# Moving the gates' exponentials between the recurrence's exponentials and its roots, and the input norm's sums and scale to fixed chunks

## The chip, the cores and the metric

One core of one Trainium2 chip runs the whole kernel in one launch. The metric is device time in microseconds (us) of one execution; the time of a kernel is the median of its runs. The engines have short names below: PE is TensorE's matmul, PEld its weight load, DVE VectorE, ACT ScalarE, POOL GpSimd and SP SyncE. Each engine works through its own instructions in the order that was fixed when the program was built; an instruction that waits holds everything behind it on that engine.

## The reference

One inference step of a one-layer hybrid decoder, for a prompt of 256 tokens and 8 sample tokens (264 columns together, model width 2048):

```python
x = x + W_out[ RGLRU-group(xn) || mLSTM-group(xn) ],  xn = RMSNorm(x)   # ONE projection xn @ w_in
x = x + CrossAttn(RMSNorm(x), memory K/V)     # 4 heads, 256 memory tokens
x = x + SwiGLU(RMSNorm(x))
y = RMSNorm_final(x)
```

The two groups matter here. The recurrence (RG-LRU) takes 1024 channels through a causal convolution of width 4, two block-diagonal projections with sigmoids (r and i), and then

```python
log_a = -RG_C * r * softplus(-lam);  a = exp(log_a)
mult = sqrt(max(1 - exp(2 * log_a), 0))
h[t] = a[t] * h[t-1] + mult[t] * (i[t] * xr[t])          # a scan over the tokens
```

The mLSTM group has 4 heads. Its input and forget gates (logi, logf = log_sigmoid) become a running sum and a running maximum over the tokens; the stabilised weights exp(...) are applied to q, k and v. For the 8 sample tokens each head reads a stored matrix memory C (128 x 256), decays it, adds a rank-one update and multiplies it with q; the new C is an output. The head outputs are normalised by a denominator and a per-head RMSNorm.

## The kernel before

**Tiling.** Activations lie transposed: channels on the 128 partitions, the 264 tokens on the free axis, so that a tile of 128 channels is 128 x 264. Weights stream from memory as blocks of 128 output channels: one *step* of the main loop (the list `steps`) is one block of 2048 weights per partition in two halves of 1024. All products of the trunk keep nearly full fp32 accuracy: a weight half (tile `raw`) is copied by ACT to a rounded high part and DVE subtracts to get the remainder (both in tile `W`, four buffers, so two steps), and each chunk of 128 input channels takes three matmuls (`mm3`: high x high, high x low, low x high). A step has 16 chunks, 48 matmuls of 264 columns.

**Steps.** Steps 0 to 3 are the first four output blocks of the recurrence's input, arranged by quarters of the input channels so that PE can begin before all of x is there; they accumulate in four PSUM banks held from the start, two with the tag `ax` (`first[0]`, `first[1]`) and two with the tag `mm` (`first[2]`, `first[3]`). There are four banks of each tag; the steps take theirs from `mm`, side work from `ax`. Steps 4 to 7 are the other four blocks of the recurrence's input, step 8 the gates (a narrow block, 32 matmuls), steps 9 to 16 q and k, 17 to 24 v, 25 to 32 the recurrence's output gate (gelu), 33 to 40 the mLSTM's output gate (sigmoid), then the output projection, the cross-attention and the feed-forward part, which the change doesn't touch.

**Input norm.** The norm's factor per token (`rstd`) is applied when a step's bank is emptied, so PE may run ahead of it, as far as banks go. `square` (line 1317) makes the squares of x on ACT in four quarters and adds them on DVE to `acc_x`. `first_norm` then lets PE sum over the partitions (`token_sums`, six small matmuls), DVE compute the inverse root (`rsqrt`, twelve small dependent instructions), PE spread the result over the partitions (`spread`, six small matmuls) and ACT copy it to `rstd`. After that `evac_first` empties the first four banks.

**Who sets the order.** A step's own code is written out in turn: the weight halves of the next step at high priority, the matmuls, then the evacuation of the step before at raised priority. Side work is written as Python generators (`rg_gen` the recurrence, `ml_gates`, `ml_prompt`, `ml_values`, `ml_heads`, `ml_sample`, `ml_norm`), each with a priority number; `pump` lets them go on after each step, lowest number first, as long as the planner's running prices of DVE and ACT (`price_dve`, `price_act`) stay under PE's price plus `SLACK`. `yield STEP` gives up until the next step. A negative priority runs regardless. A list scheduler then places the instructions of each engine from this text, by priority and its own idea of when each is ready; `tc.issue_after(ins)` forces what it encloses behind `ins` in the order of `ins`'s engine, without a wait for its end.

**Drips.** `later(f, after=n)` hands over small PE work: `drip` is called after every chunk of a projection and issues one waiting function once n chunks have gone by; the next chunk is put behind it with `issue_after`. A function's own countdown begins only when it is at the head of the list.

**The chain of the side work.** `rg_gen` takes one channel block per step: convolution, then in the next step the two projections and sigmoids; then sixteen exponentials (two per block), the products, two square roots over four blocks each, eight scans, and the output DMAs on POOL. `ml_gates` starts when step 8 is emptied: one exponential, a logarithm as a series of some fourteen DVE instructions (`log1p`), two scans, a 4 x 16 exponential (`x16`), a few small PE transposes and products, and the exponential `emc`. In the kernel before, its first exponential stands behind the recurrence's last sigmoid (`rg["last"]`) and `x16` behind the recurrence's second root (`rg["root"]`). `ml_sample` begins when the gates are done: it writes its rows to memory and reads them back spread over the partitions, and then works through 32 units (4 heads x 8 samples), each two ACT products, one DVE update of C and two DVE dot products. `ml_norm` follows when heads and samples are done; its sums (24 small matmuls) are drips too.

ACT keeps one set of function tables at a time; sigmoid, exponential, square root and gelu each bring an `ACT_TABLE_LOAD` in this kernel when the one before was of another set.

Of the kernel before, what the change touches and what calls it, by code (L numbers as in the profile page):

```python
# [17 lines left out]
P = 128  # L18
# [4 lines left out]
N = T + NS  # L23
# [60 lines left out]
def layer_kernel(ctx: ExitStack, tc, xT, memT, vec, wrg, w_in, w_out, w_q, w_k, w_v, w_o,  # L84
# [138 lines left out]
    st = {}  # L223
# [51 lines left out]
    def drip(all=False):  # L275
        while drips and (all or drips[0][0] <= 0):
            k = drips[0]
            with tc.high_priority():
                st["drip"] = k[1].pop(0)()
            if not k[1]:  # L280
                drips.pop(0)
            if not all:
                return
        if drips:
            drips[0][0] -= 1
# [61 lines left out]
    def spread(ps, c, n=N):  # L347

        for j in range(2 if n == T else 3):
            lo, hi = (j * P, j * P + P) if j < 2 else (T, N)  # L350
            pe.matmul(ps[:, lo:hi], c[j].to_broadcast([P, P]), ident[:, P - (hi - lo):], start=True, stop=True)

    def rstd_from(acc, y, n, keep=None):

# [100 lines left out]

    def evac_rgx(n):
        def f(ps):
            if n == 0:
                rg["xr"] = Arr(RGB)
            z = B([P, 2, 292])  # L460
            zi = z[:, 0, :]
            dve.memset(zi[:, 0:3], 0.0)
            smp = zi[:, 259:291].rearrange("p (b j) -> p b j", j=4)
            hist = V("cst", n * 24, 24).rearrange("p (b j) -> p b j", j=3)
            act.activation(smp[:, :, 0:3], hist, AF.Copy)
            dve.tensor_mul(zi[:, 3:259], ps[:, :T], rstd[:, :T])
            dve.tensor_mul(smp[:, :, 3:4], ps[:, T:N].rearrange("p (b j) -> p b j", j=1),
                           rstd[:, T:N].rearrange("p (b j) -> p b j", j=1))
            rg["z", n] = z
            rg["zn"] = n + 1  # L470
        return f

    def rg_conv(n):
# [15 lines left out]
    def rg_gen():  # L489
        wr = [B([P, 8, P]), B([P, 8, P])]  # L490
        for j in range(2):
            sp.dma_start(wr[j], wrg[:, j * 8: j * 8 + 8, :])
        r, ig = Arr(RGB), Arr(RGB)
        for n in range(RGB):
            while rg["zn"] <= n:
                yield STEP
            rg_conv(n)
            yield STEP
            for t, j, b in ((r, 0, "ba"), (ig, 1, "bx")):
                ps = bank("ax")  # L500
                pe.matmul(ps[:, :N], wr[j][:, n, :], rg["xr"](n), start=True, stop=True)
                last = act.activation(t(n), ps[:, :N], AF.Sigmoid, bias=V(b, n))
            yield 0.1
        yield STEP
        xr, c = rg["xr"], rg["c"]
        e2 = Arr(RGB)

        rg["last"] = last
        for q in range(2):
            for n in range(4 * q, 4 * q + 4):  # L510
                with tc.issue_after(last.ins):
                    act.activation(e2(n), r(n), AF.Exp, scale=c[:, 8 + n: 9 + n])
                    le = act.activation(r(n), r(n), AF.Exp, scale=c[:, n: n + 1])
            dve.tensor_scalar(e2.tile(q), e2.tile(q), 1.0, -1.0, op0=OP.min, op1=OP.add)
            dve.tensor_mul(ig.tile(q), ig.tile(q), xr.tile(q))
            yield 2.0
        for q in range(2):
            with tc.issue_after(le.ins):
                rg["root"] = act.activation(e2.tile(q), e2.tile(q), AF.Sqrt, scale=-1.0)
            dve.tensor_mul(ig.tile(q), ig.tile(q), e2.tile(q))  # L520
            yield 1.2
        h = Arr(RGB)
        rg["h"] = h
        for n in range(RGB):
            dve.tensor_tensor_scan(h(n)[:, :T], r(n)[:, :T], ig(n)[:, :T], 0.0, op0=OP.mult, op1=OP.add)
            yield 0.6
        h0 = V("h0", 0, 64).rearrange("p (n b) -> p n b", b=NS)
        for q in range(2):
            hq, rq_, iq = (t.tile(q)[:, :, T:N] for t in (h, r, ig))
            dve.tensor_mul(hq, rq_, h0[:, 4 * q: 4 * q + 4, :])  # L530
            dve.tensor_add(hq, hq, iq)
            act.activation(hlast[:, 4 * q: 4 * q + 4, :], h.tile(q)[:, :, T - 1: N], AF.Copy)
        pool_e.dma_start(o_h, hlast)
        pool_e.dma_start(o_cp, cpo)
        pool_e.dma_start(o_cs, cso)
        yield 0.3
# [49 lines left out]
    def ml_gates():  # L586
        R = ml["R"]
        li, u, e, lf, b, g, M = (R(j)[0:4] for j in range(7))
        yield STEP
        dve.scalar_tensor_tensor(e, u, -1.0, u, op0=OP.mult, op1=OP.min)  # L590
        while "last" not in rg:
            yield STEP
        with tc.issue_after(rg["last"].ins):
            act.activation(e, e, AF.Exp)
        yield 0.4
        log1p(lf, e)
        yield 6.0
        dve.tensor_scalar(u, u, 0.0, None, op0=OP.min)
        dve.tensor_sub(lf, u, lf)

        one = ones[0:4, 0:1].to_broadcast([4, T])
        dve.tensor_tensor_scan(b[:, :T], one, lf[:, :T], 0.0, op0=OP.mult, op1=OP.add)
        dve.tensor_sub(g[:, :T], li[:, :T], b[:, :T])
        dve.tensor_tensor_scan(M[:, :T], g[:, :T], g[:, :T], 0.0, op0=OP.max, op1=OP.max)
        dve.tensor_add(b[:, :T], b[:, :T], M[:, :T])
        dve.tensor_scalar(M[:, :T], M[:, :T], -1.0, None, op0=OP.mult)
        dve.tensor_copy(mrow[:, 0:1], b[:, T - 1: T])

        s = slice(T, N)
        dve.tensor_add(lf[:, s], lf[:, s], V("m0", 0, 8)[0:4])  # L610
        dve.tensor_max(b[:, s], lf[:, s], li[:, s])
        dve.tensor_copy(mrow[:, 1:], b[:, s])
        x16 = e[:, 0:16]
        dve.tensor_sub(x16[:, 0:8], lf[:, s], b[:, s])
        dve.tensor_sub(x16[:, 8:16], li[:, s], b[:, s])
        pool_e.dma_start(o_m, mrow)
        yield 3.0
        while "root" not in rg:
            yield STEP
        with tc.issue_after(rg["root"].ins):  # L620
            act.activation(x16, x16, AF.Exp)
        yield STEP
        ps = bank("ax")
        i4 = ident[0:4, 0:4]
        for j in range(2):
            pe.transpose(ps[:, 64 + 4 * j: 68 + 4 * j], g[:, j * P: j * P + P], i4)
        for j, w0 in enumerate(WIN):
            pe.transpose(ps[:, 72 + 4 * j: 76 + 4 * j], b[:, w0: w0 + P], i4)
        for h in range(H):
            pe.matmul(ps[:, h * 16: h * 16 + 16], ident[0:4, h: h + 1].to_broadcast([4, P]), x16,  # L630
                      start=True, stop=True)
        act.activation(bcs, ps[:, 0:64].rearrange("p (h j) -> p h j", j=16), AF.Copy)
        act.activation(gcol, ps[:, 64:72].rearrange("p (j h) -> p j h", h=H), AF.Copy)
        act.activation(emc, ps[:, 72:84], AF.Exp, scale=-1.0)
        yield 0.1

    def evac_qk(j):
# [232 lines left out]
    def proj(src, rhs, evac, cols=2048, n=N, need=()):  # L870

        def f(i):
            ps = bank()
            w = W(i)
            nch = cols // P
            for c in range(nch):
                d = st.pop("drip", None)
                if d is None:
                    mm3(ps[:, :n], w(c), rhs(c), c == 0, c == nch - 1)
                else:  # L880
                    with tc.issue_after(d.ins):
                        mm3(ps[:, :n], w(c), rhs(c), c == 0, c == nch - 1)
                drip()
            return ps
        steps.append((src, cols, f, evac, need))
# [11 lines left out]
        return f  # L897

    def evac_first(_):
        for n in range(4):  # L900
            evac_rgx(n)(first[n])

    for q in range(4):
        steps.append((w_in[q], 2048, pe_first(q), evac_first if q == 3 else None, ()))
# [409 lines left out]
    def square(q):  # L1314
        s = B([P, 4, N])
        act.activation(s, xres[:, 4 * q: 4 * q + 4, :], AF.Square)
        if q == 0:
            sq["t"] = s
            return
        dve.tensor_add(sq["t"], sq["t"], s)  # L1320
        if q == 3:
            t = sq["t"]
            dve.tensor_add(t[:, 0:2, :], t[:, 0:2, :], t[:, 2:4, :])
            dve.tensor_add(acc_x, t[:, 0, :], t[:, 1, :])

    def first_norm():
        ps = bank("ax")
# [5 lines left out]
            rsqrt(v, r)  # L1333
            return i

        k = later(sums, after=8)
        while k[1]:
            yield STEP
        spread(ps, [r[:, j: j + 1] for j in range(3)])
        act.activation(rstd, ps[:, :N], AF.Copy)  # L1340
        yield 0.1

    pend = []
    for i, (src, cols, pef, evf, need) in enumerate(steps):
# [21 lines left out]
                    square(q)  # L1366
        if i == 3:
            fn = side(first_norm(), -1)
        if i == 4:
            with tc.issue_after(st["split"].ins), tc.issue_after(st["low"].ins):  # L1370
                rg_coef()
        if evf is not None:
# [120 lines left out]
```

## Time and profile before

| | before |
|---|---|
| median of 3 runs (lowest, highest) | 1569.76 us (1567.02, 1570.49) |
| the profiled execution: time, span | 1570.7 us, 1568.9 us |
| granted TensorE clock, mean over the span | 0.991 |
| PE busy, share of the span | 1541.4 us, 98% |
| DVE busy, ACT busy | 1057.5 us, 780.7 us |
| ACT_TABLE_LOAD | 10, 1283 ns each |

How to read the rows: a row of a timeline has the start in us from the span's beginning, the duration, the engine, the line, the operation, out<-in by the program's tile names, the shape and a count; in square brackets stands the idle time before it and the engine whose work ended that idle time. Nearly all rows have line L63, since the engines are wrapped in a helper that records every operation there; tiles tell them apart: `W` and `raw` are weights, `mm` and `ax` the PSUM banks, `t` and `B` working buffers, `c` small columns, `rgc` the recurrence's coefficients, `bcs` the samples' decay factors. A row of the windows view gives, for a stretch of time, its length and the busy time (and instructions) of PE, PEld, DVE, ACT and POOL, then the granted TensorE clock, the DMA engines' busy share and GB/s.

### The profile page before, as it was taken

The numbers are of one execution on the slowest core, as the hardware profiler recorded it, in microseconds if no ns is written. First come the engines' busy times: TensorE is split into PE (matmuls) and PEld (weight loads), VectorE is DVE, ScalarE is ACT, GpSimd is POOL, SyncE is SP. The second block draws the span as 40 slices with busy tenths as digits, with TensorE's granted clock in tenths as the row PEclk, the third lists the DMA queues.
The fourth block names the chain that finished last, engine by engine and source line by source line (L and its number), as shares of the span: only waits on it lengthen the run. The fifth ranks groups of instructions, "written<-read, shape, count | busy, mean of one in ns | idle before, by whom it ended". The sixth has DMA issues, their size and how long they took to land.

```text
span 1568.9 us, 30102 instructions
## 1 busy us (share of the span) xinstructions
PE 1541.4 (98%) x12094; PEld 1506.0 (96%) x12094; DVE 1057.5 (67%) x1996; ACT 780.7 (50%) x1227; POOL 123.1 (8%) x190
## 2 busy tenths in 40 slices
PE   9999997999999999999999999999999999999997
PEld 9999997999999888889999999999999999999997
DVE  7957777788699999886665555545555555555554
ACT  7464664565455566555444444333444433444463
POOL 0000210000123243320000000000000000000000
PEclk9999998999999999999999999999999999999998
DMA  8536795556688888955555555555555555555563
GB/s 294 184 129 199 249 319 173 175 175 202 232 331 317 333 289 281 332 179 175 180 180 180 188 183 181 187 182 182 188 180 183 187 183 183 185 183 184 162 180 104
DMA packets 92171, 326.00 MB, mean 208 GB/s; under 512 B 10784, under 2 KB 11216, under 8 KB 92032
## 3 DMA queue, kind: packets, MB, share of 16 engines
q1 hardware_dynamic: 76464, 270.44, 51.5%
q0 software_dynamic: 15136, 53.16, 9.5%
q8 instruction: 94, 1.54, 0.4%
q10 hardware_dynamic: 432, 0.50, 0.1%
q14 instruction: 45, 0.37, 0.1%
HBM read 312.78 MB, written 11.28 MB: 207 GB/s over the span
## 4 chain that ended last, share of the span: by engine, by line
PE 95%; DVE 2%; ACT 1%; DMA 1%; issue 0%; DVEq 0%; ACTq 0%
PE mm L63 90%; PE ax L63 5%; DVE B L63 1%; ACT B L63 1%; DVE W L63 1%; ACT W L63 1%; DMA xres<-xT 0%; DVE t L63 0%; DMA vecs<-vec 0%; ACT L63 0%; ACT t L63 0%; DVE xres L63 0%; DVE c L63 0%; ACT rstd L63 0%; DVE acc_x L63 0%
## 5 line engine op out<-in xcount | busy, mean ns | idle before, releaser
L63 PE MATMUL mm<-B,W 128*128 128x264 f32 (+2 forms) x11008 | 1371.9, 286 | 15.6 <-DVE t L63 9.0
L63 PEld LDWEIGHTS mm<-B,W 128*128 128x128 f32 x11008 | 1348.3, 189 | 28.4 <-ACT B L63 4.9
L63 DVE TENSOR_TENSOR W<-raw,W 128x1024 fp32r<-128x1024 f32 (+2 forms) x518 | 622.4, 1204 | 378.9 <-ACT W L63 378.0
L63 ACT ACTIVATE W<-raw 128x1024 fp32r<-128x1024 f32 (+2 forms) x518 | 536.7, 1038 | 679.3 <-PE mm L63 476.9
L63 PE MATMUL mm<-W,B 128*128 128x512 f32 x384 | 92.7, 396 | 0.0
L63 PEld LDWEIGHTS mm<-W,B 128*128 128x128 f32 x384 | 71.0, 188 | 15.9
L63 DVE TENSOR_TENSOR t<-mm,rstd 128x264 f32<-128x264 f32 x104 | 44.9, 432 | 44.0 <-PE mm L63 43.6
L1385 POOL TENSOR_TENSOR B<-B,rstd 128x264 f32<-128x264 f32 x4 | 2.8, 736 | 855.1 <-ACT rstd L63 855.1
L63 DVE TENSOR_TENSOR xres<-xres,mm 128x264 f32<-128x264 f32 x80 | 34.3, 428 | 38.6 <-PE mm L63 38.6
L63 DVE SCALAR_TENSOR_TENSOR B<-B,dw 128x256 f32<-128x256 f32 x128 | 55.6, 489 | 4.0 <-ACT dw L63 4.0
L63 DVE SCALAR_TENSOR_TENSOR dw<-B,qsm,dw 128x256 f32<-128x256 f32 x96 | 49.7, 526 | 0.4
L63 PE MATMUL ax<-B,B 128*128 128x256 f32 (+3 forms) x288 | 47.8, 308 | 0.0
L63 PEld LDWEIGHTS ax<-B,B 128*128 128x128 f32 x288 | 40.6, 190 | 3.2 <-issue 0.7
L1042 POOL TENSOR_TENSOR dr<-dw,dr 128x256 fp32r<-128x256 f32 x32 | 34.1, 1070 | 106.9 <-ACT dr L63 105.7
L63 ACT ACTIVATE B<-xres,vecs 128x264 fp32r<-128x264 f32 (+1 forms) x64 | 31.1, 503 | 3.2 <-DMA vecs<-vec 1.1
L1031 POOL DMA_DIRECT2D B<-kcT x32 | 17.3, 542 | 134.2 <-DVE B L63 124.7
L63 ACT ACTIVATE B<-t 128x264 fp32r<-128x264 f32 (+1 forms) x60 | 24.3, 410 | 4.6 <-DVE t L63 4.5
L63 ACT ACTIVATE t<-xres 128x264 f32<-128x264 f32 x45 | 18.6, 414 | 15.4 <-DVE xres L63 15.4
L63 ACT ACTIVATE t<-t 128x264 f32<-128x264 f32 (+1 forms) x61 | 24.9, 408 | 2.3 <-DVE t L63 2.0
L63 ACT ACTIVATE dw<-B,qsm 128x256 f32<-128x256 f32 x32 | 16.2, 507 | 17.8 <-DVE B L63 11.1
L63 DVE SCALAR_TENSOR_TENSOR B<-xres,vecs,B 128x264 fp32r<-128x264 f32 x48 | 22.6, 490 | 3.4 <-ACT B L63 3.4
L63 ACT ACTIVATE t<-B,B 128x128 f32<-128x128 f32 x64 | 21.5, 389 | 4.2 <-DMA B<-scr 4.2
(153 smaller groups left out, 650.3 us busy)
## 6 DMA issues: line engine op xcount, KB each, us to landing
raw<-w_gu SPq DMA_DIRECT2D x176, 512.0 KB, 3.5
raw<-w_in SPq DMA_DIRECT2D x80, 512.0 KB, 4.5
raw<-w_d SPq DMA_DIRECT2D x80, 512.0 KB, 3.6
raw<-w_out SPq DMA_DIRECT2D x32, 512.0 KB, 3.9
B<-kcT POOLq DMA_DIRECT2D x32, 512.0 KB, 8.0
raw<-w_q SPq DMA_DIRECT2D x32, 512.0 KB, 4.5
B<-vcT POOLq DMA_DIRECT2D x32, 512.0 KB, 8.5
raw<-w_k SPq DMA_DIRECT2D x32, 512.0 KB, 6.9
```

The source lines that it names most:

```text
L63: return f(*a, **k)
L1031: pool_e.dma_start(kc, kcT[h, b])
L1042: pool_e.tensor_sub(wr[:, 1], acc, wr[:, 0].bitcast(F32))
L1385: e.tensor_mul(st["y"](c), st["y"](c), r)
```

## The change

- In the gates, the first exponential no longer stands behind the recurrence's last sigmoid, and `x16` stands behind the recurrence's last exponential instead of its second root. The recurrence's roots now stand behind the gates' last exponential, `emc`; `rg_gen` waits for it with `yield STEP`.
- The squares' additions run at high priority, and their tree changes: the first three quarters are folded when the third is there, the fourth is folded by itself, and one addition joins them.
- The norm's sums are issued after 4 instead of 8 counted chunks, and the spreading, which followed freely, becomes a drip of its own after 9 more. The first chunk of every projection step is put behind the last drip issued (`st["edge"]`).
- The first four banks are emptied in the order 2, 3, 0, 1, so the two of tag `mm` first, and `rg["zn"]`, which releases the convolutions, is set after all four.
- The recurrence's coefficients (`rg_coef`) are made in step 5 instead of step 4.

```diff
@@ drip
             with tc.high_priority():
-                st["drip"] = k[1].pop(0)()
+                st["drip"] = st["edge"] = k[1].pop(0)()
@@ spread
-            pe.matmul(ps[:, lo:hi], c[j].to_broadcast([P, P]), ident[:, P - (hi - lo):], start=True, stop=True)
+            i = pe.matmul(ps[:, lo:hi], c[j].to_broadcast([P, P]), ident[:, P - (hi - lo):], start=True, stop=True)
+        return i
@@ evac_rgx
-            if n == 0:
+            if "xr" not in rg:
                 rg["xr"] = Arr(RGB)
...
-            rg["zn"] = n + 1
+            if n >= 4:
+                rg["zn"] = n + 1
@@ rg_gen
-        rg["last"] = last
...
+        rg["le"] = le
+        while "emc" not in ml:
+            yield STEP
         for q in range(2):
-            with tc.issue_after(le.ins):
-                rg["root"] = act.activation(e2.tile(q), e2.tile(q), AF.Sqrt, scale=-1.0)
+            with tc.issue_after(ml["emc"].ins):
+                act.activation(e2.tile(q), e2.tile(q), AF.Sqrt, scale=-1.0)
@@ ml_gates
-        while "last" not in rg:
-            yield STEP
-        with tc.issue_after(rg["last"].ins):
-            act.activation(e, e, AF.Exp)
+        act.activation(e, e, AF.Exp)
...
-        while "root" not in rg:
+        while "le" not in rg:
             yield STEP
-        with tc.issue_after(rg["root"].ins):
+        with tc.issue_after(rg["le"].ins):
             act.activation(x16, x16, AF.Exp)
...
-        act.activation(emc, ps[:, 72:84], AF.Exp, scale=-1.0)
+        ml["emc"] = act.activation(emc, ps[:, 72:84], AF.Exp, scale=-1.0)
@@ proj
                 d = st.pop("drip", None)
+                if c == 0:
+                    d = st.get("edge")
@@ evac_first
-        for n in range(4):
+        for n in (2, 3, 0, 1):
             evac_rgx(n)(first[n])
+        rg["zn"] = 4
@@ square
-        dve.tensor_add(sq["t"], sq["t"], s)
-        if q == 3:
-            t = sq["t"]
-            dve.tensor_add(t[:, 0:2, :], t[:, 0:2, :], t[:, 2:4, :])
-            dve.tensor_add(acc_x, t[:, 0, :], t[:, 1, :])
+        with tc.high_priority():
+            if q < 3:
+                dve.tensor_add(sq["t"], sq["t"], s)
+            if q > 1:
+                t = sq["t"] if q == 2 else s
+                dve.tensor_add(t[:, 0:2, :], t[:, 0:2, :], t[:, 2:4, :])
+                dve.tensor_add(t[:, 0, :], t[:, 0, :], t[:, 1, :])
+            if q == 3:
+                dve.tensor_add(acc_x, sq["t"][:, 0, :], s[:, 0, :])
@@ first_norm
-        k = later(sums, after=8)
+        def scale():
+            i = spread(ps, [r[:, j: j + 1] for j in range(3)])
+            act.activation(rstd, ps[:, :N], AF.Copy)
+            return i
+
+        later(sums, after=4)
+        k = later(scale, after=9)
         while k[1]:
             yield STEP
-        spread(ps, [r[:, j: j + 1] for j in range(3)])
-        act.activation(rstd, ps[:, :N], AF.Copy)
         yield 0.1
@@ main loop
-        if i == 4:
+        if i == 5:
             with tc.issue_after(st["split"].ins), tc.issue_after(st["low"].ins):
                 rg_coef()
```

## The prediction

> **What bounds the kernel now.** I first read who made TensorE (PE) wait; the PE timeline of the same stretch shows no wait before 8 us that matters here and none between 278 us and the end part, so whatever this change can move lies there (the longest entries; columns: total us, times, longest).
>
> ```profile
> PE mm L63 <- DVE t L63: 9.0, 3, 4.7
> PE mm L63 <- DVE B L63: 2.7, 1, 2.7
> PE mm L63 <- DVE W L63: 2.0, 1, 2.0
> ```
>
> These fall at three places. The PE timeline around each (start, us, what, count, idle before and its releaser):
>
> ```profile
> 29.05 9.28 PE L63 MATMUL mm<-B,W 128*128 128x264 f32 x76
> 38.16 0.72 PE L63 MATMUL ax<-ones,acc_x 128*128 128x1 f32 x6
> 38.75 5.05 PE L63 MATMUL mm<-B,W 128*128 128x264 f32 x40
> 44.09 0.81 PE L63 MATMUL ax<-ident,c 128*128 128x128 f32 x6 [0.29 <-DVE c L63]
> 47.57 11.04 PE L63 MATMUL mm<-B,W 128*128 128x264 f32 x77 [2.67 <-DVE B L63]
> ...
> 116.15 3.38 PE L63 MATMUL mm<-B,W 128*128 128x264 f32 x26 [0.83 <-ACT W L63]
> 121.56 18.61 PE L63 MATMUL mm<-B,W 128*128 128x264 f32 x140 [2.03 <-DVE W L63]
> ...
> 148.03 5.99 PE L63 MATMUL mm<-B,W 128*128 128x264 f32 x48
> ...
> 162.81 6.01 PE L63 MATMUL mm<-B,W 128*128 128x264 f32 x48
> ...
> 208.31 23.25 PE L63 MATMUL mm<-B,W 128*128 128x264 f32 x192
> 232.26 6.00 PE L63 MATMUL mm<-B,W 128*128 128x264 f32 x48 [0.70 <-DVE t L63]
> 241.83 0.61 PE L63 MATMUL mm<-B,W 128*128 128x264 f32 x3 [3.57 <-DVE t L63]
> 247.19 6.29 PE L63 MATMUL mm<-B,W 128*128 128x264 f32 x30 [4.75 <-DVE t L63]
> 253.32 2.73 PE L63 MATMUL ax<-ones,B 128*128 128x1 f32 x24
> 255.91 7.69 PE L63 MATMUL mm<-B,W 128*128 128x264 f32 x49
> ```
>
> Undisturbed, 192 matmuls take 23.25 us: 0.121 us each, 5.8 us for a weight step of 48. After each place PE also runs at half clock for a while (windows; the last three columns are PEclk, DMA share, GB/s):
>
> ```profile
> 47.73:51.14 3.41, 3.41 (x17) 3.41 (x17) 3.41 (x13) 0.64 (x4) 0.00 (x0) 0.50 0.46 154
> 122.82:126.23 3.41, 3.41 (x18) 3.41 (x17) 3.41 (x7) 0.46 (x1) 0.00 (x0) 0.50 0.81 243
> 242.29:252.53 10.24, 5.49 (x26) 5.37 (x25) 8.35 (x29) 6.04 (x19) 2.64 (x5) 0.50 0.57 190
> ```
>
> So each place costs its idle time plus the slow matmuls behind it. The last matmul of a group stands 0.17 us longer than its pitch, which I take off.
> - **Place 1, input norm**: idle 0.29 + 2.67 = 2.96; slow 11.04 - 0.17 - 77 x 0.121 = 1.55. Together 4.5.
> - **Place 2, recurrence**: 0.83 + 2.03 = 2.86; slow 18.61 - 0.17 - 140 x 0.121 = 1.5. Together 4.4.
> - **Place 3, end of the mLSTM samples**: 0.70 + 3.57 + 4.75 = 9.0; slow 6.29 - 0.17 - 30 x 0.121 = 2.5 and 7.69 - 0.17 - 49 x 0.121 = 1.6. Together 13.1.
>
> 22.0 us in all: the change can't win more.
>
> **The change part by part.** I sum against the profiled execution's own 1570.7 us (span 1568.9), 0.9 above the median 1569.8.
>
> *Norm at fixed chunks, banks first.* Step 4 begins after 20 of the 76 matmuls, at 29.05 + 20 x 0.121 = 31.5. There the sums came 56 matmuls later, at 38.16. Then the scale waited for the root's chain on VectorE (DVE):
>
> ```profile
> 33.97 0.43 DVE L63 TENSOR_TENSOR acc_x<-B 128x264 f32<-128x264 f32 x1
> ...
> 38.93 0.16 DVE L63 TENSOR_SCALAR c<-ax 128x3 f32<-128x3 f32 x1 [0.54 <-PE ax L63]
> ...
> 42.64 1.23 DVE L63 TENSOR_TENSOR W<-raw,W 128x1024 fp32r<-128x1024 f32 x1 [0.36 <-ACT W L63]
> 43.79 0.16 DVE L63 SCALAR_TENSOR_TENSOR c<-c,c 128x3 f32<-128x3 f32 x1
> ...
> 46.12 0.90 DVE L63 TENSOR_TENSOR B<-ax,rstd 128x256 f32<-128x256 f32 x4
> ```
>
> After the change the sums stand behind five chunks: 31.5 + 15 x 0.121 = 33.3. acc_x was ready at 34.4 (33.97 + 0.43), so PE could wait 1.1 there; the sum of squares now goes at high priority and one 1056-wide addition has left its tail, so I take 0. The root's chain took 5.0 us (38.93 to 43.95), 2.5 of them two weight remainders of 1.23 like the one at 42.64, with the recurrence's coefficients, which the diff moves a step later, between its links. Ten chunks (3.6 us) now cover it: a wait of 0 to 1.4, I take 0.3, nearer the chain without remainders. Emptying banks mm first moves them ahead of the 0.90 row; with the scale some five microseconds earlier, step 6 finds a bank free anyway. Worth 4.5 - 0.3 = **4.2** (4.5 at best; with both waits at their ends, 1.1 + 1.4, it is 2.0). The additions of the squares keep nearly their work: nothing, under cover of PE's step 3, which has its weights.
>
> *Gates between exponentials and roots.* ScalarE (ACT) and DVE at place 2:
>
> ```profile
> 100.80 0.83 ACT L63 ACTIVATE B<-ax,vecs 128x264 f32<-128x264 f32 x2
> 101.66 1.28 ACT L63 ACT_TABLE_LOAD   x1
> 102.95 2.96 ACT L63 ACTIVATE B<-B,rgc 128x264 f32<-128x264 f32 x7
> ...
> 108.16 1.04 ACT L63 ACTIVATE W<-raw 128x1024 fp32r<-128x1024 f32 x1
> ...
> 110.85 1.28 ACT L63 ACT_TABLE_LOAD   x1
> ...
> 115.06 2.94 ACT L63 ACTIVATE W<-raw 128x1024 fp32r<-128x1024 f32 x3
> ...
> 116.26 2.42 DVE L63 TENSOR_TENSOR_SCAN B<-B,B 128x256 f32<-128x256 f32 x4
> ...
> 120.30 3.47 DVE L63 TENSOR_TENSOR W<-raw,W 128x1024 fp32r<-128x1024 f32 x3
> ```
>
> A step eats a weight copy each 2.9 us. The exponentials let one through at 108.16; the root's table load and two roots held the next ones until three ran together at 115.06, and the scans and the gates' logarithm stood before their remainders at 120.30. Now the roots stand behind the gates' last exponential (emc), which planning order puts two steps behind the recurrence's exponentials. Emc itself waits for PE's small gate matmuls; behind it in ACT's queue are the weight copies of that moment, which have two steps of lead. So the copies can follow at about 111, 4 us before PE missed one, and the logarithm, issued in step 10 without its wait, is off DVE before. The roots' 1.28 + 2.1 us on ACT, the products and eight scans on DVE come where the logarithm stood. I take **4.4**; it can be 0 if the crowd is only moved, and a loss of the same 4.4 if the roots' stage makes a second hole while the exponentials keep theirs. What it costs: the early gate exponential adds two table loads (to exponentials and back to sigmoids), 2 x 1.28 us. They lie in a stage like this one, where ACT (fourth pair, 2.87 of 6.67 us) has 3.8 free, so 0; without that cover, 2.6 less a weight copy's 2.9 of lead, still 0.
>
> ```profile
> 73.70:80.37 6.67, 6.67 (x55) 6.54 (x53) 5.83 (x10) 2.87 (x5) 0.00 (x0) 1.00 0.58 185
> ```
>
> [...]
>
> *What the earlier gates do to place 3.* The samples (32 units of one DVE update, two ACT products, two dots) can't start before the gates are done:
>
> ```profile
> 147.90 0.19 ACT L63 ACTIVATE emc<-ax 128x12 f32<-128x12 f32 x1
> ...
> 166.01 0.48 DVE L63 SCALAR_TENSOR_TENSOR B<-B,bcs,t 128x256 f32<-128x256 f32 x1 [1.89 <-ACT t L63]
> ...
> 245.88 0.48 DVE L63 SCALAR_TENSOR_TENSOR B<-B,bcs,t 128x256 f32<-128x256 f32 x1
> ```
>
> The first unit came 3.2 us into step 23 (162.81). By the planner's order the gates end three steps sooner, but the roots and scans now use up step 18, so I move the units two steps: to 3.2 us into step 21. That step began at 148.03 and loses 4.2 + 4.4 = 8.6: start at 142.6, which is S = 23.4 us sooner. POOL's queue moves with it: the recurrence's three output DMAs now go ahead of the samples' row write instead of long before it, so late scans would hold the samples too; that is one of the things that make S smaller. But the steps that need them move too. The head norm's sums are issued in the third step behind the last units: step 33 before, step 31 now, which begins at 208.31 + 144 x 0.121 - 8.6 = 217.1, first chunk done 217.5. The sums' input was ready between the last unit, 247.2, and 253.3; I take 250. With the units' pace kept, PE waits 250 - 23.4 - 217.5 = 9.1 us. And the new edge on each first chunk forbids what PE did at 247.19, thirty matmuls of the next step ahead of the sums. (On other steps that edge costs nothing: the instruction it names is long issued.) With a slow stretch between the 1.6 and 4.1 above, say 3, place 3 costs 12.1 against 13.1: **1.0** won. The ends: 13.1 won if the units catch up; 10 lost if S is only some 12 (9.1 + 11.4 + 3 against 13.1).
>
> Sum: 4.2 + 4.4 + 1.0 = 9.6, so 1570.7 - 9.6 = **1561**.
>
> **The rivals.**
> - *Units catch up.* Between 140.4 and 162.8 DVE was busy in 10.7 of 22.4 us, while in 201 to 247 it had 36 of 46. If units fill that idle time, place 3 vanishes: 1570.7 - 8.6 - 13.1 = 1549. Against it: the copies of weights, paced by PE, stand between units in both queues.
>
> ```profile
> 140.36:162.81 22.45, 22.45 (x187) 21.76 (x186) 10.74 (x20) 11.38 (x18) 4.46 (x9) 1.00 0.53 174
> ...
> 201.00:247.00 46.00, 37.17 (x301) 36.38 (x299) 36.15 (x112) 27.61 (x65) 4.62 (x9) 0.95 0.83 292
> ```
>
> - *Place 2 only moves.* The sixteen exponentials and their load stay in one run; PE misses a weight there or at the roots: 1570.7 - 4.2 - 1.0 = 1565.5. The like if the norm does not do what it says, sums and scale waiting at their chunks instead.
> - *Slower: the edge holds PE at the head norm's sums.* The mechanism is the 250 - S - 217.5 above, with no matmuls let past. With 3 us of slow clock it eats all gains when the wait is 18.7 us, that is S under 13.8. Roots and scans ahead of the units, or the samples' reload of rows by DMA, would have to hold them two steps. At S = 9: wait 23.5, 26.5 against 13.1, so 1570.7 - 8.6 + 13.4 = 1575.5.
> - *Nothing nets out*, 1570: gains and a smaller hold cancel.
>
> **How the numbers follow.** Forecast (1557 to 1565) 0.40, units catch up 0.22, place 2 moves 0.18, edge holds 0.15, nothing 0.05. No change is within 0.2%, 3.1 us of 1569.8, which is what a measurement can tell. Faster: the first two and 0.10 of the third, 0.72; same: 0.08 and the 0.05, 0.13; slower 0.15. The range for 8 in 10 goes from 1548 to 1573: it takes in the catching up but for its lowest tail, and the edge until its middle.
>
> **What would show it.** Right, step by step: six sums behind 15 matmuls of step 4 and no idle over 1.4 us nor half clock at 40 to 55; no wait at 105 to 125, weight copies never three in a row behind roots; two more table loads, one pair near 75; first unit near 143; PE still idle near 217 to 227, released by the sums' input. Wrong: a wait at 33 (sums late), roots and scans with a PE wait behind them, or a first unit after 152.

## The result and the profile after

The changed kernel takes 1560.39 us (median of 6 runs, 1558.76 to 1562.52); before, measured beside it, 1570.07 us (6 runs). The ratio is 0.9941, 95% interval 0.9928 to 0.9954. The profiled execution took 1558.76 us, span 1557.1; it is the quickest of the six, 1.6 below the median, which I keep in mind below.

Who made PE wait in the changed kernel, up to 320 us (columns as in the prediction):

```profile
PE ax L63 <- DVE B L63: 4.1, 1, 4.1
PE mm L63 <- DVE ones L63: 1.1, 1, 1.1
PE ax L63 <- DVE acc_x L63: 1.0, 1, 1.0
PE ax L63 <- ACT W L63: 0.9, 2, 0.6
PE mm L63 <- DVE t L63: 0.7, 1, 0.7
PE ax L63 <- DVE c L63: 0.3, 1, 0.3
```

Its PE timeline at the three places:

```profile
28.50 4.37 PE L63 MATMUL mm<-B,W 128*128 128x264 f32 x35
33.84 0.83 PE L63 MATMUL ax<-ones,acc_x 128*128 128x1 f32 x6 [0.96 <-DVE acc_x L63]
34.53 3.85 PE L63 MATMUL mm<-B,W 128*128 128x264 f32 x30
38.64 0.81 PE L63 MATMUL ax<-ident,c 128*128 128x128 f32 x6 [0.26 <-DVE c L63]
39.30 18.46 PE L63 MATMUL mm<-B,W 128*128 128x264 f32 x152
...
102.33 17.62 PE L63 MATMUL mm<-B,W 128*128 128x264 f32 x144
...
140.71 5.99 PE L63 MATMUL mm<-B,W 128*128 128x264 f32 x48
...
194.44 23.25 PE L63 MATMUL mm<-B,W 128*128 128x264 f32 x192
218.40 0.60 PE L63 MATMUL mm<-B,W 128*128 128x264 f32 x3 [0.70 <-DVE t L63]
223.12 1.41 PE L63 MATMUL ax<-ones,B 128*128 128x1 f32 x6 [4.11 <-DVE B L63]
```

Place 1 is down to two waits, 0.96 and 0.26, with no half clock; place 2 is gone (144 matmuls without a break where there were two waits); at place 3 PE does the three matmuls of one chunk and then stands before the heads' sums, where it stood before banks. Half clock is left there only, up to the end part (windows of the changed kernel, columns as before):

```profile
222.59:232.84 10.25, 9.72 (x45) 9.75 (x46) 7.09 (x29) 3.21 (x9) 2.28 (x5) 0.50 0.76 260
```

(The prediction saw no wait between 278 us and the end part. There is one, of 0.81 us at 363.56 in the kernel before; it stands unchanged at 351.53 in the changed one.)

It helps to place events by the step that PE is in, counted by its matmuls with tile W in the trace (22.0 is the start of step 22; times in us). The last column is the time from the end of step 30 to the end of step 40, so what place 3 costs shows in it. The kernels of the experiments are below.

| kernel | emc | first unit | last unit | heads' sums | end of step 30 | end of step 40 | step 30 to 40 |
|---|---|---|---|---|---|---|---|
| before | 147.9 (21.0) | 166.0 (23.5) | 245.9 (33.1) | 253.3 (33.7) | 225.8 | 303.8 | 78.0 |
| after | 121.5 (18.0) | 147.7 (22.0) | 221.5 (31.1) | 223.1 (31.1) | 217.7 | 291.8 | 74.1 |
| norm part alone | 142.8 (21.0) | 160.4 (23.5) | 240.8 (33.1) | 244.5 (33.1) | 220.7 | 303.0 | 82.3 |
| gates part alone | 126.2 (18.0) | 154.8 (22.3) | 229.1 (31.1) | 230.7 (31.1) | 225.3 | 299.6 | 74.3 |
| late gate exponential | 133.1 (20.0) | 159.3 (23.9) | 239.7 (33.1) | 243.4 (33.1) | 219.6 | 301.6 | 82.0 |
| roots back | 121.6 (17.6) | 148.0 (21.4) | 229.0 (31.1) | 230.9 (31.1) | 222.5 | 300.8 | 78.4 |
| sums a step later | 121.7 (18.0) | 149.4 (22.1) | 223.3 (31.5) | 226.2 (32.0) | 219.5 | 288.1 | 68.6 |

So of 12.0 us at the end of step 40, 8.1 are there at the end of step 30 (places 1 and 2) and 3.9 come from place 3. These are two single executions, 11.9 us apart in time (1570.7 and 1558.76); the medians are 9.7 apart.

### The profile page after: what moved, and what is told of

It is laid out like the page before. It is cut to its first block, busy times and chain, and to the rows that moved or that the text cites. A ratio compares the mean times of both kernels' runs of the same rounds, so it can differ in the third digit from the quotient of the medians.

```text
span 1557.1 us, 30109 instructions
## 1 busy us (share of the span) xinstructions
PE 1537.7 (99%) x12094; PEld 1502.1 (96%) x12094; DVE 1055.1 (68%) x1998; ACT 781.7 (50%) x1229; POOL 123.1 (8%) x190
## 4 chain that ended last, share of the span: by engine, by line
PE 96%; DVE 2%; ACT 1%; DMA 1%; issue 0%; DVEq 0%; ACTq 0%
PE mm L63 91%; PE ax L63 5%; DVE B L63 1%; DVE W L63 1%; ACT W L63 0%; DMA xres<-xT 0%; DMA vecs<-vec 0%; ACT B L63 0%; ACT t L63 0%; DVE c L63 0%; DVE xres L63 0%; DVE acc_x L63 0%; DVE t L63 0%; ACT rstd L63 0%; DVEq L1482 0%
## 5 line engine op out<-in xcount | busy, mean ns | idle before, releaser
L63 ACT ACTIVATE B<-xres,vecs 128x264 fp32r<-128x264 f32 (+1 forms) x64 | 31.1, 503 | 3.6 <-DMA vecs<-vec 1.5
L63 ACT ACTIVATE t<-B,B 128x128 f32<-128x128 f32 x64 | 21.4, 389 | 4.8 <-DMA B<-scr 4.8
```

What stands on the lines that cost most here:

```text
L63: return f(*a, **k)
```

## The experiments

All comparisons are with the kernel before on the same chip; intervals are 95%.

**Norm part alone.** The gates, exponentials and roots as before; everything on the norm, the drips and the banks as changed.

```diff
-        act.activation(e, e, AF.Exp)                  # gates
+        while "last" not in rg:
+            yield STEP
+        with tc.issue_after(rg["last"].ins):
+            act.activation(e, e, AF.Exp)
...
-        with tc.issue_after(rg["le"].ins):            # x16
+        with tc.issue_after(rg["root"].ins):
...
-            with tc.issue_after(ml["emc"].ins):       # roots
+            with tc.issue_after(le.ins):
```

> The changed kernel with its gates part undone: first gate exponential behind the last sigmoid, roots straight behind the recurrence's exponentials, x16 behind the roots; the norm's chunks, the edge, the squares and the bank order stay. Theory (three places that add up): place 1 is gone (PE waits near 33 of 1 us, no half clock at 45 to 55, 3.3 us better than before), place 2 stays at some 110 to 121 with 2 to 3 us of wait and a half-clock stretch, place 3 stays, with PE now held at the heads' sums instead of at banks, 13 to 17 us. Time 1567 to 1571, so little or nothing of the 9.7 us. Rival (the norm part is the main gain, place 2 was an after-effect of the late norm): place 2 gone as well, time 1561 to 1564.

1570.87 us, ratio 1.0008 (0.9999 to 1.0016): nothing. Its waits, and PE at place 3:

```profile
PE ax L63 <- DVE B L63: 6.8, 1, 6.8
PE mm L63 <- DVE t L63: 4.3, 2, 3.6
PE mm L63 <- DVE W L63: 2.0, 1, 2.0
PE mm L63 <- DVE ones L63: 1.1, 1, 1.1
PE mm L63 <- ACT W L63: 1.1, 2, 0.8
PE ax L63 <- DVE acc_x L63: 1.0, 1, 1.0
...
236.73 1.00 PE L63 MATMUL mm<-B,W 128*128 128x264 f32 x3 [3.57 <-DVE t L63]
244.48 1.41 PE L63 MATMUL ax<-ones,B 128*128 128x1 f32 x6 [6.75 <-DVE B L63]
```

Place 1 was cured. The end of step 30 is 5.1 us earlier: 3.3 by place 1, and most of the rest because behind the waits at place 2, 0.83 and 2.03 us as before, no half clock shows in this execution (140 matmuls in 17.05 us, 18.61 in the kernel before). All but less than 1 us was lost again by the end of step 40. The samples were not what PE had outrun: their last unit came 5.1 us earlier too, and the first wait for a bank is the same 3.57 us. What differs stands behind it. The heads' sums follow the first chunk of step 33 directly, where the kernel before does thirty matmuls of the next step first; PE waits 6.75 us for them, where it waited 4.75 for a bank, and the half-clock stretch is 20.48 us long instead of 10.24 and 3.41. Steps 31 to 40 took 82.3 us instead of 78.0. The time came out as the theory had it. Whether it is the edge that puts the sums first here, as the prediction says, no run tests.

**Gates part alone.** The kernel before with only the three edits on the gates and the roots.

> The kernel before with the gates part alone. Theory: place 1 stays as before (waits 0.29 and 2.7 us, one half-clock stretch), place 2 is gone, place 3 shrinks because the samples' last unit ends some 20 us sooner, and without the edge PE may pass matmuls ahead of the heads' sums: 1570.1 less 4.4 and 3 to 6, so 1560 to 1563. Rival (place 3 shrank through the norm part): place 3 still 13 us, time 1565 to 1566.

1564.10 us, ratio 0.9968 (0.9956 to 0.9981), 5.9 us. A little short of the theory: place 2 is gone and the last unit is 16.8 us earlier, but the trace has a new wait of 1.70 us before PE's transposes at 169.66, with 21 slow matmuls behind it (3.89 us, 2.78 in the changed kernel), and at place 1 the 77 matmuls behind the wait for a bank took 12.20 us instead of 11.04. The parts alone do not add: nothing and 5.9, 9.7 together. In one order they do: the gates part wins 5.9, and the norm part behind it another 3.7 (1564.10 to 1560.39), near the 3.3 of place 1.

This kernel has no edge, and yet PE waits at the heads' sums for the same 4.11 us:

```profile
226.00 0.60 PE L63 MATMUL mm<-B,W 128*128 128x264 f32 x3 [0.70 <-DVE t L63]
230.72 1.28 PE L63 MATMUL ax<-ones,B 128*128 128x1 f32 x6 [4.11 <-DVE B L63]
```

**Edge for the input norm alone.**

```diff
-                st["drip"] = st["edge"] = k[1].pop(0)()
+                st["drip"] = d = k[1].pop(0)()
+                if "ng" not in ml:            # until the head norm exists
+                    st["edge"] = d
```

> The changed kernel, but only the input norm's drips set the edge; the heads' sums no longer hold the next step's first chunk. Theory (the edge holds PE at the heads' sums): in place of the 4.1 us wait PE runs some thirty matmuls of the next step, 3.6 us at full clock, and place 3 is 3 to 7 us cheaper: 1553 to 1557. Rival (a bank stands in the way anyway, as in the kernel before): PE waits for a bank instead, time 1559 to 1562.

1560.10 us, ratio 0.9941 (0.9930 to 0.9953): as the changed kernel. The order of PE's instructions came out the same as with the edge, so the edge holds nothing at the heads. The theory fell; the rival's reason (a bank) is not what the trace shows either, since the wait is still the 4.11 us for the sums' input. With the samples ending in step 31 the list scheduler puts nothing ahead of those sums, edge or not.

**No edge at all.**

```diff
-                if c == 0:
-                    d = st.get("edge")
```

> The changed kernel without the edge at the first chunk of each step; the sums after 4 and the scale after 9 chunks stay drips. Theory (the edge is what fixes the place): the list scheduler puts chunks of step 5 ahead of the norm's scale again, the scale comes late, and a wait of 1 to 3 us for banks with a half-clock stretch returns near 45: place 1 is 2 to 4.5 us worse, but since a gain at place 1 was given back at place 3 in the kernel with the norm part alone, the time may be 1560 to 1565. Rival (the smaller counts alone do it): no wait at place 1 beyond the 1.2 us of the changed kernel, 1559 to 1561.

1561.60 us, ratio 0.9952 (0.9939 to 0.9964). Here the edge does what it is there for. Without it the sums come at 37.80 again, and the bank wait is back:

```profile
37.80 0.72 PE L63 MATMUL ax<-ones,acc_x 128*128 128x1 f32 x6
43.16 0.73 PE L63 MATMUL ax<-ident,c 128*128 128x128 f32 x6
46.67 18.08 PE L63 MATMUL mm<-B,W 128*128 128x264 f32 x137 [2.31 <-DVE B L63]
```

In the medians it costs 1.2 us, about as much as its waits at place 1 are longer (2.31 against 0.96 and 0.26). Place 3 gives nothing back: the waits there are the same 0.70 and 4.11 us, and the 39 matmuls behind the heads' sums took 7.04 us, where 37 took 5.99 in the changed kernel. The profiled execution, the slowest of the five, is 4.2 us behind that of the changed kernel. The expected range held.

**Old bank order.** `for n in range(4)` in `evac_first`.

> The changed kernel with the first four banks emptied in the old order, 0 to 3. The prediction gave the new order no worth of its own, since step 6 finds a free bank once the scale is early. Theory: 1559 to 1562, no PE wait for a bank at 40 to 50. Rival (the mm banks first are what cures place 1): a bank wait of 0.5 to 1 us at 45 and, if it brings the half clock, 2 to 3 us more than 1560.4.

1559.86 us, ratio 0.9939 (0.9926 to 0.9951), and no wait at 40 to 50. The order is worth nothing once the scale is early.

**Late gate exponential.** Only the first gate exponential goes back behind the last sigmoid; the roots still follow emc.

```diff
-        act.activation(e, e, AF.Exp)
+        while "last" not in rg:
+            yield STEP
+        with tc.issue_after(rg["last"].ins):
+            act.activation(e, e, AF.Exp)
```

> The changed kernel, but the gates' first exponential stands behind the recurrence's last sigmoid again, as before; the roots still wait for emc. The question is what cured place 2 and what moves place 3. Theory (the roots' move cures place 2; the gates' end sets place 3): no PE wait at 105 to 120, since the weight copies still follow the exponentials at once; but the logarithm comes about 25 us later, the gates end near 140 instead of 121, the samples start later by 10 to 20 us, and PE waits longer at the heads' sums: 1564 to 1570. Rival (the early logarithm cured place 2 by leaving DVE free): a PE wait for W on DVE of about 2 us and a half-clock stretch near 110 to 120 come back, 4.4 us on top. Third possibility (the start of the gates does not matter): 1559 to 1562.

1569.49 us, ratio 0.9996 (0.9987 to 1.0004). The most telling run. Places 1 and 2 are both cured:

```profile
96.75 33.42 PE L63 MATMUL mm<-B,W 128*128 128x264 f32 x276
...
226.03 6.01 PE L63 MATMUL mm<-B,W 128*128 128x264 f32 x48 [0.71 <-DVE t L63]
235.61 1.00 PE L63 MATMUL mm<-B,W 128*128 128x264 f32 x3 [3.57 <-DVE t L63]
243.36 1.41 PE L63 MATMUL ax<-ones,B 128*128 128x1 f32 x6 [6.75 <-DVE B L63]
```

276 matmuls run without a break where place 2 was, though the logarithm stands on DVE there again: it was the roots' move that cured place 2. But emc comes in step 20 instead of 18, the units run to step 33.1 again, and the 6.2 us that PE had won by step 30 shrink to 2.2 by step 40, although the last unit came 6.2 us earlier as well. The waits at place 3 are those of the norm part alone, with the sums straight behind the first chunk, and so is the half-clock stretch of 20.48 us. Two cured places are worth nothing while the samples end in step 33 and the sums stand in front.

**Roots back.** The other half: the early exponential stays, roots straight behind the exponentials, x16 behind the second root.

> The changed kernel with the roots straight behind the recurrence's exponentials and x16 behind the second root, as before; the early gate exponential and the norm part stay. Theory (the early exponential is what moves the samples; the roots' move alone cures place 2): PE waits for W near 110 to 120 again, 2 to 3 us with a half-clock stretch, emc comes 3 to 8 us later than in the changed kernel, and the units' end sets the time: 1561 to 1565. Rival (only both together help): the samples end as late as with the norm part alone, 1568 to 1571. Third possibility: place 2 stays cured, since the logarithm is off DVE: 1559 to 1561.

1566.99 us (1565.33 to 1574.83), ratio 0.9993 (0.9980 to 1.0006). My estimate was too low by 2 us and the table shows that its reason was off: emc comes at 121.6 and the first unit at 148.0, as in the changed kernel within 0.3 us, and the last unit in the same step 31.1, but 7.5 us later. It is PE that is late: 4.8 us by the end of step 30, with place 2 partly back (a wait of 1.18 us for a weight until 118.65, and eight transposes at 121.16 that took 1.97 us, 1.03 in the changed kernel) and a wait of 1.43 at 175.52. At place 3 PE then waits 3.57 us for a bank instead of 0.70, and 4.08 for the sums. So an early end of the gates is not enough; the units also have to be dealt out over the steps as the changed order does it. Here three of them come after the end of step 30 instead of one, and the evacuation that frees the bank stands behind the first of the three. Why this order leaves more of them, I did not settle.

**Sums a step later, in two kernels; and 32 chunks.** First the changed kernel with

```diff
-        k = later(*[lambda h=h: sums(h) for h in range(H)])
+        k = later(*[lambda h=h: sums(h) for h in range(H)], after=16)
```

> The changed kernel with sixteen counted chunks ahead of the heads' sums, so that they come a step later; the edge stays. Theory: the sums' input is ready at 223 and PE comes to the sums at about 224, so the 4.1 us wait and the 10.24 us half-clock stretch behind it (4.9 us) go, and what is left of place 3 is the 0.7 us wait for a bank, perhaps a few us more of it: 1551 to 1555. Rival (the samples still set the pace, the wait moves to banks or to the evacuation of the output gate's first block, which needs the normalised heads): 1558 to 1562.

1553.69 us, ratio 0.9899 (0.9884 to 0.9913): 6.7 us better than the changed kernel. PE now does all of step 31 while the samples end:

```profile
220.24 6.01 PE L63 MATMUL mm<-B,W 128*128 128x264 f32 x48 [0.70 <-DVE t L63]
226.22 2.14 PE L63 MATMUL ax<-ones,B 128*128 128x1 f32 x18
228.22 2.25 PE L63 MATMUL mm<-B,W 128*128 128x264 f32 x12
230.27 1.27 PE L63 MATMUL ax<-ones,B 128*128 128x1 f32 x6
...
229.10:235.93 6.83, 6.83 (x33) 6.83 (x32) 5.56 (x22) 3.75 (x8) 0.00 (x0) 0.50 0.99 364
```

The last row is from its windows. A half-clock stretch follows the sums although PE waited for nothing there. I tried the four heads' sums apart, `after=4` for each head behind the first:

> The heads' sums a step later as in the kernel with sixteen counted chunks more, and the four heads' six one-column matmuls apart by five chunks each instead of nearly together. That kernel had a half-clock stretch of 6.83 us right behind the sums although PE waited no more than 0.7 us there. Theory (a dense group of one-column matmuls counts as idle for the clock): apart, they leave no half clock, 3.4 us less than 1553.7: 1549 to 1552. Rival (the 0.7 us bank wait, or the waits of other engines, bring the half clock): the stretch stays, 1552 to 1555; and if the later last sums hold the spread and the output gate's first block, PE waits there and the time is 1555 or more.

1550.83 us, ratio 0.9882 (0.9867 to 0.9897), and the 53 matmuls behind the sums at full pace (6.61 us, 8.68 in the kernel before this one). But the list scheduler had put the sums together again: the order on PE is the same as in the kernel before this one, 18 matmuls, 12 of the step, 6. So *apart* was not tried, and this is the same order on another chip; the two ratios overlap. The same order shows 6.83 us of half clock in one profiled execution (1555.06 us) and full pace in the other (1550.89 us); why, no run here shows. The earlier of the two kernels also took 1550.67 us in one of its four runs.

With `after=32`:

> The changed kernel with the heads' sums two steps later instead of one. Theory: one step was enough, since the sums' input was ready at 223 to 225 and PE came to the sums at 225 to 226; nothing is left to win there and the normalised heads still come in time for the output gate: 1550 to 1554. Rival (a step too late: the output gate's first evacuations wait for the heads and banks fill up): 1555 to 1562.

1554.69 us, ratio 0.9899 (0.9883 to 0.9914): as with 16, and 0.7 above the expected range. But the sums stand where they stood with 16, behind the 48 matmuls of step 31 (18 of them at 226.54, 12 matmuls of the next step, 6 more); the spreading of their result comes 31 matmuls later. So two steps were not tried either.

**The kernel before with its sums later.** `after=16` and nothing else.

> The kernel before with the heads' sums sixteen chunks later and nothing else. Theory (the samples' end against PE's step is what place 3 costs; in the kernel before the samples run to step 33.1 and the banks wait for evacuations behind them): the sums' place was not what PE waited for, since its waits at 241.83 and 247.19 were for banks; the time stays at 1568 to 1571, or gets worse by up to 4 us as the sums then hold the output gate's blocks. Rival (the sums' place alone is worth what it was worth in the changed kernel): 1562 to 1565.

1567.91 us, ratio 0.9989 (0.9980 to 0.9998), 0.1 below the expected range. The first wait for a bank, 3.57 us, stays. The second, 4.75, is gone, since PE does all of step 33 ahead of the sums, and waits of 1.70 and 0.30 us for the sums' input stand there instead; PE still runs slowly at place 3: the 48 matmuls behind the wait of 3.57 took 7.38 us and the 23 behind the sums 5.41, at the undisturbed 0.121 us each 5.8 and 2.8. The same edit is worth 6.7 us behind the early gates and 2.2 without them.

**Idle-looking work.** To see whether one-column matmuls bring the half clock where PE does not wait, groups of 12, 24, 36 and 48 of them were added in the output projection (steps 51 to 54); no result uses them.

```diff
+    def dense(n):
+        ps = bank("ax")
+        for j in range(n):
+            k = pe.matmul(ps[:, j: j + 1], ones, ones[:, 0:1], start=True, stop=True)
+        return k
```

> The kernel with the heads' sums later and apart, with four groups of idle work added in the quiet stretch of the output projection (steps 51 to 54): 12, 24, 36 and 48 one-column matmuls back to back, which no result uses. PE waits for nothing there. Theory (one-column matmuls count as idle for the clock): behind the groups of 36 and 48, perhaps 24, stands a half-clock stretch of 3.41 us each; the added work is 120 x 0.11 = 13 us and the half clock 1.7 us per stretch, so 1566 to 1569. Rival (only waits bring the half clock): the granted clock stays full near 300 to 350, and the time is 1550.8 + 13 = 1564.

1601.59 us, ratio 1.0207. The scheduler put all 120 in one group (two records each), which took 46 us instead of my 13. PE waits for nothing, and the granted clock drops from 1.00 to 0.50 5.3 us into the group:

```profile
329.88 46.38 PE L63 MATMUL ax<-ones 128*128 128x1 f32 x240
...
329.88:335.18 5.30, 5.30 (x51) 5.30 (x49) 1.97 (x3) 1.21 (x3) 0.00 (x0) 1.00 0.56 189
335.18:350.30 15.12, 15.12 (x73) 15.12 (x73) 0.00 (x0) 0.00 (x0) 0.00 (x0) 0.50 0.00 1
350.30:379.55 29.25, 29.25 (x137) 29.25 (x138) 2.20 (x7) 2.13 (x6) 0.00 (x0) 0.50 0.00 1
379.55:385.00 5.45, 5.45 (x47) 5.45 (x47) 5.45 (x16) 5.45 (x13) 0.00 (x0) 1.00 0.00 0
```

It comes back at 379.55, 3.3 us after the group's end at 376.26, when 3.0 us of the next step's matmuls are done. So the clock fell in this long group without a wait; how short a group already does it, this run does not say.

## Why the prediction was right, and where its steps failed

The time was right: 1561 forecast, 1560.4 measured, won at the places that were named. That the sum fits so closely is partly luck: place 1 gave 0.9 less than its term and place 3 some 2.4 more, and in the two profiled executions, from which the terms are read, the gain is 11.9 us and not 9.7.

- **Place 1** was to save 4.2. It saved 2.96 + 1.55 - 0.96 - 0.26 = 3.3. The mechanism was right; the mis-sized term is the wait for acc_x, taken as 0 with a bound of 1.1: it is 0.96. Raised priority did not carry the additions past the weight remainders, one of which still stands before the last one:

```profile
30.96 0.78 DVE L63 TENSOR_TENSOR B<-B 128x264 f32<-128x264 f32 x2
32.21 1.23 DVE L63 TENSOR_TENSOR W<-raw,W 128x1024 fp32r<-128x1024 f32 x1 [0.48 <-ACT W L63]
33.35 0.43 DVE L63 TENSOR_TENSOR acc_x<-B,B 128x264 f32<-128x264 f32 x1
```

  The root's chain met its cover of ten chunks within 0.26 us (0.3 taken), and the bank order is worth nothing, as taken.
- **Place 2** was to save 4.4 and did. The copies ran at 112.5, forecast 111, ahead of PE's need; the two extra table loads stand at 77.94 and 89.61 and nobody waits for them. The run with the late exponential shows that the roots' move is the cause; with the roots back, 1.18 us of the wait returns. The first load begins 0.02 us after the sigmoid before it ends, and the exponential stands 1.29 us behind the load's start.

```profile
77.09 0.83 ACT L63 ACTIVATE B<-ax,vecs 128x264 f32<-128x264 f32 x2
77.94 1.28 ACT L63 ACT_TABLE_LOAD   x1
79.23 0.42 ACT L63 ACTIVATE B<-B 4x264 f32<-4x264 f32 x1
...
112.52 2.94 ACT L63 ACTIVATE W<-raw 128x1024 fp32r<-128x1024 f32 x3
```

- **Place 3** was to cost 12.1, and costs 0.70 + 4.11 and half of 9.72 us at half clock, 4.9: 9.7. The structure was right to the step: units ending in step 31, PE at the sums at 218.4 + 0.6 (forecast 217.5), held there by their input. Three terms were off. The first unit came at 147.7, not 142.6. PE's lead at step 21 was 7.3 us and not 8.6, and the way from the row write to the first unit, which waits for the read-back in both kernels, took 11.9 us (from 135.77) instead of 9.5 (from 156.53). The pace was not kept: DVE was busy 14.95 of 22.45 us in the once half-idle stretch, and the units needed 74 us instead of 80 from first to last, or 9.1 of PE's steps instead of 9.5. That looks like the rival *units catch up* at work in part, and it made up for the late start: the sums' input was ready at 223.1, forecast 226.6, and the wait was 4.11, forecast 9.1. And the half clock cost 4.9, taken as 3. The first row is of the kernel before, the others of the changed one.

```profile
165.28 0.70 ACT L63 ACTIVATE t<-B,B 128x128 f32<-128x128 f32 x2 [2.60 <-DMA B<-scr]
...
146.94 0.69 ACT L63 ACTIVATE t<-B,B 128x128 f32<-128x128 f32 x2 [4.84 <-DMA B<-scr]
147.66 0.49 DVE L63 SCALAR_TENSOR_TENSOR B<-B,bcs,t 128x256 f32<-128x256 f32 x1 [4.79 <-ACT t L63]
...
140.36:162.81 22.45, 22.45 (x171) 20.89 (x170) 14.95 (x46) 14.06 (x28) 6.42 (x12) 1.00 0.94 302
```

- **The step that failed is the edge at the heads' sums**: "the new edge on each first chunk forbids what PE did at 247.19". PE waits there without the edge too (gates part alone) and its order is the same when the edge ends with the input norm. The order of the kernel before, with thirty matmuls ahead of the sums, came from the list scheduler's own plan. For the changed kernel the slower rival, which rested on the edge, has lost its mechanism. In the two kernels whose samples end in step 33 the sums do stand in front and steps 31 to 40 take some 4 us longer than before; both have the edge, and no run takes it out of them.
- **What the sum got right without saying it**: the 8.6 us of places 1 and 2 are in S and in PE's arrival at 217.5, so they cancel in the wait at place 3, and earlier PE does not wait longer. The runs bear this out. Six kernels have the samples' end in step 31 and the sums behind its first chunk. In five of them (changed, gates part alone, edge for the input norm alone, old bank order, no edge; not in the one with the roots back) PE comes to the sums between 219.0 and 226.6 and waits 4.11 us, since their input is ready 5.4 us after the end of step 30 in each. In the changed kernel the chain is this: PE's last matmuls of step 30, ending at 217.7, release a weight copy on ACT; its remainder on DVE, the last unit and the additions for the sums stand behind it.

```profile
217.74 1.06 ACT L63 ACTIVATE W<-raw 128x1024 fp32r<-128x1024 f32 x1 [1.23 <-PE mm L63]
218.83 1.23 DVE L63 TENSOR_TENSOR W<-raw,W 128x1024 fp32r<-128x1024 f32 x1 [0.36 <-ACT W L63]
221.48 0.48 DVE L63 SCALAR_TENSOR_TENSOR B<-B,bcs,t 128x256 f32<-128x256 f32 x1 [0.15 <-ACT t L63]
222.54 1.11 DVE L63 TENSOR_TENSOR B<-B,t 128x264 f32<-128x264 f32 x3
```

- **What the sum did not see**: the price of place 3 depends on the step in which the samples end and on what stands ahead of the sums. Steps 31 to 40 took 78.0 us before, 82 with the samples ending in step 33 and the sums in front, 74 with the samples ending in step 31 (78.4 with the roots back and its longer wait for a bank). So with late gates one place cured is worth 0 and both are worth 0, and with early gates the norm part is worth 3.7. Neither half of the gates part does it alone: the early exponential alone ends the gates as early (121.6) and leaves 1567.0, the roots' move alone cures place 2 and leaves 1569.5. The squares' new tree, the two counts and the coefficients' step were not tried one by one.

## What to carry to other kernels

Before counting a removed wait as won, follow PE to the next place on the path and see whether the changed program leaves that place as it was: here two cured waits were lost again in full at a third place whose order had changed, until the chain that feeds it ended two steps earlier. Measure such a place from one fixed step of PE to another; its price then stands apart from what was won ahead of it. When that chain has been moved, look at where its consumer is issued: putting the sums one step later, behind work that was ready, was worth another 6.7 us for one argument. A helper that fixes an order is worth testing place by place, since a planner may give the same order without it.

## What the hardware showed that I had not expected

In the run with the added work the clock of PE fell without a wait: PE was never idle there, the granted clock went from 1.00 to 0.50 5.3 us into the one-column matmuls (329.88 to 335.18), and it stayed at 0.50 for 44.4 us, until 379.55. In the kernel before, a stretch of 3.41 us begins at 255.94, right behind 24 such sums (253.32, 2.73 us) and without a wait; whether the sums brought it was not tested by itself. And waits of 1.70 to 2.04 us had slow matmuls behind them in some traces and not in others. The wait of 2.03 us before 121.56 in the kernel before was followed by a stretch of 3.41 us at 122.82, and in the gates part alone 21 matmuls behind a wait of 1.70 us (until 169.66) took 3.89 us, where the changed kernel took 2.78. The same wait of 2.03 us with the norm part alone (until 118.00) had none behind it, 140 matmuls in 17.05 us, and neither had one of 2.04 with the late exponential (until 184.70), 36 matmuls in 4.58 us. So in these traces the length of a wait alone does not tell whether slow matmuls follow; what does, no run here shows.
